# Splitting the first two chunks of the second feed-forward product inside the last group of the first, and loading the next rows one set at a time

## The chip, the cores and the metric

The kernel runs on one core of one Trainium2 chip. The metric is device time in microseconds, the median of three runs. A profile of one further execution was taken with the hardware profiler; its span runs from the first instruction of the program to the last. Engines go by these names: PE or TensorE (matmuls), DVE or VectorE, ACT or ScalarE, POOL or GpSimd, and SP, whose queue issues nearly all DMAs of this kernel.

## What is computed

One layer of a transformer over 2048 latent tokens of width 1024, in 32-bit floats: attention and a gated MLP branch, merged, then a feed-forward sub-layer. The change is in the feed-forward:

```
h2 = modulate(x, norm2_g, sh2, sc2)              # rmsnorm(x, g) * (1 + scale) + shift
x  = x + g2 * (square(relu(h2 @ w_ff1)) @ w_ff2) # w_ff1: 1024 x 4096, w_ff2: 4096 x 1024
```

## The kernel before, in words

**Precision.** Every 32-bit operand `a` of a product is split into a high part in a shorter format (`fp32r`), which ScalarE casts, and the remainder `a - high`, which VectorE subtracts. A product is then three matmuls: high by high, high by low, low by high (`product`, lines 1286 to 1288).

**Seven products instead of eight.** Both feed-forward products work on 2 x 2 blocks of operands and form them from seven block products (Strassen-Winograd); the sums and differences of blocks are made on VectorE. The results accumulate in PSUM banks; some of the seven add on to a bank that another has filled, once that bank was read or rewritten.

**Two blocks.** The 2048 tokens go in two blocks of 1024 (`blk` 0 and 1). For each, `ff1` runs 16 groups (`ff1_group`), each of 7 products of 12 matmuls; the seven combined activations of each group go out to DRAM (`ao_d`, lines 1314 to 1344). During block 0, `w2_late` also forms the seven combinations of the second weights, a slice per group, and stores them (`w2o_d`, `w2_ops`, lines 1259 to 1273); the last group does two slices. Then `ff2` runs 7 x 8 = 56 steps: for each of the seven products, in the order 0, 1, 5, 6, 4, 2, 3, eight chunks `c`, each with four token tiles `t`, 24 matmuls in all.

**A chunk's way.** `ff2_fetch` loads the two operands of a chunk from DRAM (line 1382), 512 KB each, into two buffers of the tag `f4`. `ff2_split` casts each into a further `f4` buffer (ScalarE, line 1391) and subtracts in place (VectorE, line 1392). A chunk thus takes four buffers once split; there are 12 (`"f4": 12`). The weights of a first group use the same tag. Before the loop of `ff2`, chunk 0 is split and chunks 1 and 2 are being loaded; step `n` begins by splitting chunk `n + 1`, then issues the load of chunk `n + 3`, then multiplies chunk `n`.

**After the eighth chunk of a product** (`c == NCH - 1`), `take` evicts each token tile's sum: product 0, 5 and 6 are copied out by ScalarE; product 1 is multiplied by the gate on VectorE (`leave`), after which ScalarE writes product 0's sum back into the bank (line 1437); products 4 and 2 are added to a running sum on VectorE and multiplied by the gate; product 3 is multiplied. Products 0, 1, 5, 6 and 3 share one set of four banks, 4 and 2 the other. `leave` puts the remaining work on the output rows (adding the residual, loaded at line 1413, and the store at line 1426) on a list `late`, from which the next steps take two entries each.

**The side work.** While block 0 is in `ff2`, `h_ops(1, ...)` prepares the first products' operands for block 1: it loads rows of `x` in four sets of four DMAs (`h_fetch`, line 1063, tag `f8`), scales them on VectorE by the inverse root mean square (`h_rstd`, `h_scaled`, line 1070), transposes them on TensorE (`h_turn`, line 184) and makes the seven combinations. It is a generator that advances once at the end of each step. 

**What sets the order.** A planner of the framework orders each engine's instructions by its own costs. `order` adds links that hold parts of it to the order in which the program writes them: all of `ff2` on every engine (`steady`, and `loads` for SP), single stretches (`pins`), and for each tag the order in which buffers are first written. The groups of `ff1` are left to the planner. Engines work through their queues in order, so an instruction that waits holds all that stands behind it.

Of the kernel before, what the change touches and what calls it, by code (L numbers as in the profile page):

```python
# [10 lines left out]
F32R = mybir.dt.float32r  # L11
I32 = mybir.dt.int32
AF = mybir.ActivationFunctionType
ALU = mybir.AluOpType
# [6 lines left out]
KC = D // P  # L21
# [8 lines left out]
TB = 512  # L30
# [16 lines left out]
def f32(ap):  # L47
    return ap.bitcast(F32)
# [20 lines left out]
class Kern:  # L69
# [1012 lines left out]
    def h_ops(self, blk, ops):  # L1082
        nc = self.nc
        add, sub = ALU.add, ALU.subtract
        at = self.here()
        rb = self.h_rstd(blk)
        self.pins.append(range(at, self.here()))
        x = [self.h_fetch(blk, kk) for kk in range(2)]
        yield
        for kk in range(KC // 2):  # L1090
            self.h_scaled(x[kk], rb)
            yield
            raw = {}
            for j in range(2):
                for i in range(2):
                    raw[i, j] = self.h_turn(x[kk], kk, i, j)
                if j and kk + 2 < KC // 2:
                    x.append(self.h_fetch(blk, kk + 2))
                yield
            tt = nc.vector.tensor_tensor  # L1100
            r00, r01, r10, r11 = (raw[i, j] for i in range(2) for j in range(2))
            s1 = self.sb("f2", [TB])
            ops[0][kk] = self.halves(kk, 0, r00)
            tt(out=s1, in0=r10, in1=r11, op=add)
            tt(out=r10, in0=r00, in1=r10, op=sub)
            tt(out=r00, in0=s1, in1=r00, op=sub)
            ops[5][kk] = self.halves(kk, 5, r00)
            yield
            ops[1][kk] = self.halves(kk, 1, r01)
            tt(out=r00, in0=r01, in1=r00, op=sub)  # L1110
            ops[6][kk] = self.halves(kk, 6, r10)
            yield
            ops[4][kk] = self.halves(kk, 4, s1)
            ops[3][kk] = self.halves(kk, 3, r11)
            ops[2][kk] = self.halves(kk, 2, r00)
            yield
# [230 lines left out]
    def ff1(self, blk, h, extra):  # L1347
        w = {0: {}}
        first = self.w1_ops(0, w[0])
        rest = iter(()) if blk else self.h_rest()  # L1350
        if blk == 0:
            for it in (first, rest, rest, first):
                next(it)
        else:
            for _ in first:
                pass
        for g in range(NG):
            nxt = iter(())
            if g + 1 < NG:
                w[g + 1] = {}  # L1360
                nxt = self.w1_ops(g + 1, w[g + 1])
            else:
                raw = self.ff2_fetch(blk, 0, 0)
                self.ready = [self.ff2_split(raw)]
                self.raws = [self.ff2_fetch(blk, 0, 1)]
            more = extra(g)
            for n, _ in enumerate(self.ff1_group(blk, g, w.pop(g), h)):
                next(rest, None)
                if n == 3:
                    next(first, None)  # L1370
                next(nxt, None)
                next(more, None)
            for _ in nxt:
                pass
            for _ in more:
                pass

    def ff2_fetch(self, blk, p, c):
        out = []
        for src in (self.ao_d[blk][p][c], self.wo_d[p][c]):  # L1380
            l = self.sb("f4", [2, TB], F32R)
            self.nc.sync.dma_start(f32(l), src.rearrange("s p c -> p s c"))
            out.append(l)
        return out

    def ff2_split(self, raw):
        nc = self.nc
        out = []
        for l in raw:
            h = self.sb("f4", [2, TB], F32R)  # L1390
            nc.scalar.copy(h, f32(l))  # L1391
            nc.vector.tensor_tensor(out=l, in0=f32(l), in1=f32(h), op=ALU.subtract)  # L1392
            out.append((h, l))
        return out

    def ff2(self, blk, side):
        nc = self.nc
        add, mult = ALU.add, ALU.mult
        begin = self.here()
        ready = self.ready  # L1400
        raws = self.raws + [self.ff2_fetch(blk, 0, 2)]
        late = []

        def tt(out, in0, in1, op):
            nc.vector.tensor_tensor(out=out, in0=in0, in1=in1, op=op)

        goes = {1: (0, 0), 4: (1, 1), 2: (0, 1), 3: (1, 0)}
        u2, u3, xs = ([None] * TT for _ in range(3))

        def residual(p, t):  # L1410
            i, j = goes[p]
            xs[t] = self.sb("f2", [TB])
            nc.sync.dma_start(
                xs[t], self.x1_d[2 * blk + i][t * P : (t + 1) * P, j * TB : (j + 1) * TB]
            )

        def leave(p, t, src):
            i, j = goes[p]
            row = (2 * blk + i) * TB + t * P
            cs = slice(j * TB, (j + 1) * TB)  # L1420
            c, x = self.sb("f2", [TB]), xs[t]
            tt(c, src, self.g2b[:, cs], mult)

            def rest():
                tt(c, c, x, add)
                nc.sync.dma_start(self.out[0, row : row + P, cs], c)

            late.append(rest)

        def take(p, t):  # L1430
            ps = banks[p][t]
            if p == 0:
                u2[t] = self.sb("f2", [TB])
                nc.scalar.copy(u2[t], ps)
            elif p == 1:
                leave(p, t, ps)
                nc.scalar.copy(ps, u2[t])
            elif p in (5, 6):
                u = u2 if p == 5 else u3
                u[t] = self.sb("f2", [TB])  # L1440
                nc.scalar.copy(u[t], ps)
            elif p in (4, 2):
                u = u3[t] if p == 4 else u2[t]
                tt(u, u, ps, add)
                leave(p, t, u)
            else:
                leave(p, t, ps)

        order = (0, 1, 5, 6, 4, 2, 3)
        steps = [(p, c) for p in order for c in range(NCH)]  # L1450
        banks = {}
        for n, (p, c) in enumerate(steps):
            if raws:
                ready.append(self.ff2_split(raws.pop(0)))
            if n + 3 < len(steps):
                raws.append(self.ff2_fetch(blk, *steps[n + 3]))
            (ah, al), (wh, wl) = ready.pop(0)
            fresh = p in (0, 4)
            if c == 0 and fresh:
                new = [self.bank([TB]) for _ in range(TT)]  # L1460
                for other in (0, 1, 5, 6, 3) if p == 0 else (4, 2):
                    banks[other] = new
            if c >= NCH - TT and p in goes:
                residual(p, c - (NCH - TT))
            for t in range(TT):
                if late and t % 2 == 0 and c < NCH - 1:
                    late.pop(0)()
                tok = slice(t * P, (t + 1) * P)
                a = [(ah[:, s, tok], al[:, s, tok]) for s in range(2)]
                b = [(wh[:, s], wl[:, s]) for s in range(2)]  # L1470
                self.product(banks[p][t], a, b, fresh and c == 0)
                if c == NCH - 1:
                    take(p, t)
            next(side, None)
        for f in late:
            f()
        for _ in side:
            pass
        self.loads.append(range(begin, self.here()))
        self.steady.append(range(begin, self.here()))  # L1480
# [336 lines left out]
```

## Time and profile before

| what | value |
|---|---|
| median of three runs | 3013.18 us (3012.45 to 3016.2) |
| the profiled execution | 3012.34 us, of which the span is 3010.6 us |
| granted TensorE clock, mean | 0.999 |
| TensorE busy (matmuls) | 2971.5 us, 99% of the span |
| VectorE busy | 2024.5 us, 67% |
| ScalarE busy | 1353.1 us, 45% |
| DMA | 485.53 MB, 161 GB/s over the span |
| last group of first products, block 0 | 2050.47 to 2070.04 us |
| second products, block 0 and block 1 | from 2070.04 and from 2697.96 us |

Times in the profile are microseconds from the start of the span. A row of a timeline shows start, duration, engine (with q: its instruction queue), line, operation and tiles (written <- read, buffer numbers left out); in square brackets stands how long the engine was idle before and what ended the wait. A matmul is shown with a modelled end: each takes 0.39 us in the records though they start every 0.23 us.

### The profile page before, as it was taken

To read this page: it belongs to the slowest core of one execution; us is meant where nothing else is said; L and a number is where in the kernel's file an instruction comes from. 1 tells how busy PE (TensorE), PEld (TensorE's weight loads), DVE (VectorE), ACT (ScalarE), POOL (GpSimd) and SP (SyncE) were. 2 spreads that over 40 slices of the span, in tenths; PEclk is the share of its full clock that TensorE was granted. 3 is DMA by queue.
4 is the path that set the end of the run, shared out by engine and by line. 5 is a ranking of instruction groups with operands and counts; after the bars stand their busy time and mean duration, and the time that the engine had idled before them with its cause. 6 is when DMAs were issued, how large, how long until landed. Compare 5 with 4: busy or idle time off the path is not lost.

```text
span 3010.6 us, 39824 instructions
## 1 busy us (share of the span) xinstructions
PE 2971.5 (99%) x14973; PEld 2300.4 (76%) x14973; DVE 2024.5 (67%) x2989; ACT 1353.1 (45%) x2041; POOL 564.9 (19%) x420
## 2 busy tenths in 40 slices
PE   7999999999999999999999999999999999999999
PEld 5888888887655656556888878887788888888887
DVE  5848566585777788886655688776755766654455
ACT  4444435342655555554322355443543344444442
POOL 0000000000888899980000000000000000000000
PEclk9999999999999999999999999999999999999999
DMA  7474646643100000003755549888766544446665
GB/s 239 124 219 118 225 137 198 180 138 98 36 15 12 15 19 22 29 26 131 234 174 179 173 151 328 310 305 312 243 203 226 183 154 154 154 148 219 209 218 195
DMA packets 329123, 485.53 MB, mean 161 GB/s; under 512 B 28825, under 2 KB 161217, under 8 KB 328930
## 3 DMA queue, kind: packets, MB, share of 16 engines
q1 hardware_dynamic: 325090, 478.40, 48.1%
q10 hardware_dynamic: 3840, 4.59, 0.4%
q8 instruction: 117, 1.92, 0.3%
q14 instruction: 76, 0.62, 0.1%
HBM read 348.56 MB, written 134.35 MB: 160 GB/s over the span
## 4 chain that ended last, share of the span: by engine, by line
PE 95%; DVE 2%; DMA 2%; ACT 1%; issue 1%; SPq 0%; DVEq 0%; ACTq 0%
PE b L1287 13%; PE b L1288 13%; PE b L1286 13%; PE b L178 11%; PE b L180 11%; PE b L179 11%; PE b L1689 9%; PE b L1709 8%; PE b L1645 2%; PE b L184 2%; DMA w<-in_w_mod 1%; PE b L1751 0%; PE b L288 0%; DMA f<-x_d 0%; DVE ts L1656 0%
## 5 line engine op out<-in xcount | busy, mean ns | idle before, releaser
L1392 DVE TENSOR_TENSOR f<-f,f 128x1024 fp32r<-128x1024 f32 x224 | 264.5, 1221 | 252.7 <-ACT f L1391 252.4
L1656 DVE TENSOR_REDUCE ts<-b 128x1 f32<-128x512 f32 x512 | 311.6, 682 | 105.6 <-PE b L1645 105.5
L1287 PE MATMUL b<-f,f 128*128 128x512 f32 x896 | 350.6, 391 | 5.5 <-DVE f L1392 5.3
L1391 ACT CAST f<-f 128x1024 fp32r<-128x1024 f32 x224 | 224.8, 1052 | 287.3 <-PE b L1287 274.8
L1286 PE MATMUL b<-f,f 128*128 128x512 f32 x896 | 350.2, 391 | 1.3 <-ACT f L1391 1.3
L1288 PE MATMUL b<-f,f 128*128 128x512 f32 x896 | 349.4, 390 | 0.0
L1689 PE MATMUL b<-t,t 64*128 64x512 f32 x2304 | 330.7, 400 | 0.0
L1689 PEld LDWEIGHTS b<-t,t 64*128 64x128 f32 x2304 | 226.1, 184 | 69.2 <-issue 26.1
L1732 POOL TENSOR_TENSOR ac<-ac,p 128x512 f32<-128x512 f32 x204 | 269.0, 1353 | 43.4 <-ACT p L1699 43.4
L1732 POOL TENSOR_TENSOR ac<-ac,t 128x512 f32<-128x512 f32 x146 | 233.2, 1627 | 0.0
L1699 ACT ACTIVATE p<-b 128x512 f32<-128x512 f32 x384 | 206.8, 599 | 48.2 <-PE b L1689 41.4
L1287 PE MATMUL b<-hl,f 128*128 128x512 f32 x576 | 224.4, 390 | 1.8 <-DVE hl L1049 1.8
L1288 PE MATMUL b<-hl,f 128*128 128x512 f32 x576 | 224.1, 389 | 0.0
L1286 PE MATMUL b<-hl,f 128*128 128x512 f32 x576 | 224.1, 389 | 0.0
L150 DVE TENSOR_TENSOR w<-w,w 128x1024 fp32r<-128x1024 f32 x120 | 146.7, 1223 | 113.5 <-ACT w L146 85.7
L178 PE MATMUL b<-t,w 128*128 128x512 f32 x512 | 203.2, 397 | 0.4 <-DVE ts L1651 0.3
L1287 PEld LDWEIGHTS b<-f,f 128*128 128x128 f32 x896 | 168.5, 188 | 44.1 <-DVE f L1392 9.5
L180 PE MATMUL b<-t,w 128*128 128x512 f32 x512 | 199.7, 390 | 0.0
L179 PE MATMUL b<-t,w 128*128 128x512 f32 x512 | 199.5, 390 | 0.0
L1286 PEld LDWEIGHTS b<-f,f 128*128 128x128 f32 x896 | 168.6, 188 | 37.3 <-ACT f L1391 2.4
L1288 PEld LDWEIGHTS b<-f,f 128*128 128x128 f32 x896 | 168.6, 188 | 34.7
L146 ACT CAST w<-w 128x1024 fp32r<-128x1024 f32 x120 | 125.9, 1049 | 146.5 <-DMA w<-in_w_in 116.8
(234 smaller groups left out, 6013.3 us busy)
## 6 DMA issues: line engine op xcount, KB each, us to landing
w<-in_w_in SPq DMA_DIRECT2D x120, 512.0 KB
ao_d<-f SPq DMA_DIRECT2D x224, 256.0 KB
f<-ao_d SPq DMA_DIRECT2D x112, 512.0 KB
f<-w2o_d SPq DMA_DIRECT2D x112, 512.0 KB
f<-in_w_ff SPq DMA_DIRECT2D x48, 1024.0 KB
w2o_d<-f SPq DMA_DIRECT2D x112, 256.0 KB
md<-in_w_mod SPq DMA_DIRECT2D x32, 512.0 KB
f<-x_d SPq DMA_DIRECT2D x64, 256.0 KB
```

Of the source, the lines that this page charges most:

```text
L178: mm(ps, sh, mh, start=start, stop=False, skip_group_check=skip)
L179: mm(ps, sh, ml, start=False, stop=False, skip_group_check=skip)
L180: mm(ps, sl, mh, start=False, stop=stop, skip_group_check=skip)
L1286: mm(ps, wh, hh, start=start and k == 0, stop=False, skip_group_check=True)
L1287: mm(ps, wh, hl, start=False, stop=False, skip_group_check=True)
L1288: mm(ps, wl, hh, start=False, stop=k == len(w) - 1, skip_group_check=True)
L1391: nc.scalar.copy(h, f32(l))
L1392: nc.vector.tensor_tensor(out=l, in0=f32(l), in1=f32(h), op=ALU.subtract)
L1656: nc.vector.tensor_reduce(out=self.mx[:, t, h, c : c + 1], in_=ps[h], axis=AX.X, op=ALU.max)
L1689: self.nc.tensor.matmul(ps[h], keys[h], q[rows[h]], start=n == 0, stop=n == len(steps) - 1, skip_group_check=True,)
L1709: nc.tensor.matmul(self.o[h * HD : (h + 1) * HD, :], k.V[c][:, i, self.kv * HD : (self.kv + 1) * HD], pt[h], start=j == 0, stop=j == NKT - 1,)
L1732: nc.gpsimd.tensor_tensor(out=self.acc[e][:, h], in0=old[:, h], in1=pt[h], op=ALU.add)
```

## The change

Three things are changed, with no change in what is computed.

- In the last group of `ff1` the planner no longer orders the instructions of TensorE, VectorE and ScalarE: the whole group joins `steady`. Inside it a new generator, `ff2_first`, loads the second products' chunks 0 and 1 after the group's first product and splits one operand of them (`ff2_half`: a cast and a subtraction) after each of the next four. `ff2` so begins with two chunks ready and none loaded; its loop, which splits one chunk and loads one per step, is as before, and so is the number of buffers.
- `h_ops` loads one set of rows at a time: the first when it starts, each further one after the scaling of the set before it. Before, two sets were loaded at the start and each further one two ahead. The inverse root mean square of block 1 is computed in group 2 of block 0's first products, not at the start of `h_ops`.
- In `ff2` the side work does not advance at the end of a step in which output rows are still on the list `late`.

```diff
@@ def h_ops(self, blk, ops)
-        at = self.here()
-        rb = self.h_rstd(blk)
-        self.pins.append(range(at, self.here()))
-        x = [self.h_fetch(blk, kk) for kk in range(2)]
+        rb = self.rb1
+        x = [self.h_fetch(blk, 0)]
         yield
         for kk in range(KC // 2):
             self.h_scaled(x[kk], rb)
+            if kk + 1 < KC // 2:
+                x.append(self.h_fetch(blk, kk + 1))
             yield
             raw = {}
             for j in range(2):
                 for i in range(2):
                     raw[i, j] = self.h_turn(x[kk], kk, i, j)
-                if j and kk + 2 < KC // 2:
-                    x.append(self.h_fetch(blk, kk + 2))
                 yield
@@ def ff1(self, blk, h, extra)
         for g in range(NG):
-            nxt = iter(())
+            begin = self.here()
             if g + 1 < NG:
                 w[g + 1] = {}
                 nxt = self.w1_ops(g + 1, w[g + 1])
             else:
-                raw = self.ff2_fetch(blk, 0, 0)
-                self.ready = [self.ff2_split(raw)]
-                self.raws = [self.ff2_fetch(blk, 0, 1)]
+                nxt = self.ff2_first(blk)
+            if g == 2 and blk == 0:
+                self.rb1 = self.h_rstd(1)
...
             for _ in more:
                 pass
+        self.steady.append(range(begin, self.here()))
+
+    def ff2_first(self, blk):
+        self.ready, self.raws = [], []
+        raws = [self.ff2_fetch(blk, 0, c) for c in range(2)]
+        for raw in raws:
+            got = []
+            for l in raw:
+                yield
+                got.append(self.ff2_half(l))
+            self.ready.append(got)
+
+    def ff2_half(self, l):
+        h = self.sb("f4", [2, TB], F32R)
+        self.nc.scalar.copy(h, f32(l))
+        self.nc.vector.tensor_tensor(out=l, in0=f32(l), in1=f32(h), op=ALU.subtract)
+        return h, l
@@ def ff2_split(self, raw)
-        nc = self.nc
-        out = []
-        for l in raw:
-            h = self.sb("f4", [2, TB], F32R)
-            nc.scalar.copy(h, f32(l))
-            nc.vector.tensor_tensor(out=l, in0=f32(l), in1=f32(h), op=ALU.subtract)
-            out.append((h, l))
-        return out
+        return [self.ff2_half(l) for l in raw]
@@ def ff2(self, blk, side)
-            next(side, None)
+            if not late:
+                next(side, None)
```

## The prediction

> **What bounds the kernel now.** I read the page, then what TensorE waited for, then, around those waits, the timelines of the four queues.
>
> ```profile
> span 3010.6 us, 39824 instructions
> PE 2971.5 (99%) x14973; PEld 2300.4 (76%) x14973; DVE 2024.5 (67%) x2989; ACT 1353.1 (45%) x2041; POOL 564.9 (19%) x420
> ```
>
> TensorE is the bound, so only two things count: waits of TensorE that vanish, and waits that are new. In the part that the change touches (two blocks, each 16 groups of first products and 56 steps of second products) its timeline shows these waits:
>
> ```profile
> 2076.06 0.50 PE L1286 MATMUL b<-f,f 128*128 128x512 f32 x1 [0.42 <-ACT f L1391]
> 2078.38 0.50 PE L1287 MATMUL b<-f,f 128*128 128x512 f32 x1 [1.81 <-DVE f L1392]
> 2084.86 0.50 PE L1287 MATMUL b<-f,f 128*128 128x512 f32 x1 [0.70 <-DVE f L1392]
> 2091.13 1.09 PE L184 MATMUL b<-ident,f 128*128 128x128 f32 x8 [0.75 <-DVE f L1070]
> 2093.40 0.50 PE L1287 MATMUL b<-f,f 128*128 128x512 f32 x1 [0.94 <-DVE f L1392]
> 2181.43 0.50 PE L1286 MATMUL b<-f,f 128*128 128x512 f32 x1 [0.88 <-ACT f L1391]
> 2182.88 0.50 PE L1287 MATMUL b<-f,f 128*128 128x512 f32 x1 [0.95 <-DVE f L1392]
> 2704.83 0.50 PE L1287 MATMUL b<-f,f 128*128 128x512 f32 x1 [0.94 <-DVE f L1392]
> ```
>
> The bracket is idle time after a modelled end; as these ends overlap, each wait costs some 0.2 us more. Block 0's entry into the second products loses 4.6 + 5 x 0.2 = 5.6 us, the place at 2181 1.8 + 0.4 = 2.2, block 1's entry 1.1. After the second of them the clock was halved for one stretch:
>
> ```profile
> 2180.20:2183.60 3.40, 1.57 (x6) 0.82 (x5) 3.15 (x5) 3.40 (x6) 0.00 (x0) 1.00 0.45 172
> 2183.60:2187.00 3.40, 3.40 (x10) 2.63 (x9) 3.40 (x6) 2.29 (x4) 0.00 (x0) 0.50 0.79 240
> 2074.40:2077.80 3.40, 1.74 (x7) 0.89 (x5) 3.40 (x5) 1.61 (x2) 0.00 (x0) 1.00 0.97 369
> 1802.80:1821.90 19.10, 19.10 (x86) 15.80 (x85) 15.24 (x22) 11.02 (x17) 0.00 (x0) 1.00 0.85 296
> ```
>
> Columns: stretch, length, busy TensorE, weight loads, VectorE, ScalarE, GpSimd, granted clock. A stretch with TensorE busy 1.57 of 3.40 us was followed by 3.4 us at 0.50; one with 1.74 was not. Half of 3.4 us is 1.7; the halved stretch runs 10 matmuls instead of the next one's 16, 6 x 0.23 = 1.4: some 1.6 us lost. So at most 5.6 + 2.2 + 1.6 + 1.1 = 10.5 us can be won.
>
> **The steady step.** A step is 24 matmuls; from 2742.81 to 2786.33, the starts of steps 8 and 16 of block 1, is 8 steps, 5.44 us each.
>
> ```profile
> 2050.47 0.39 PE L1286 MATMUL b<-he,f 128*128 128x512 f32 x1
> 2678.92 0.39 PE L1286 MATMUL b<-he,f 128*128 128x512 f32 x1
> 2710.40 0.39 PE L1287 MATMUL b<-f,f 128*128 128x512 f32 x1
> 2742.81 0.39 PE L1286 MATMUL b<-f,f 128*128 128x512 f32 x1
> 2786.33 0.39 PE L1286 MATMUL b<-f,f 128*128 128x512 f32 x1
> ```
>
> ```profile
> 2075.48 1.02 SPq L1273 DMA_DIRECT2D w2o_d<-f  x2
> 2076.59 0.41 SPq L1382 DMA_DIRECT2D f<-ao_d  x1
> 2078.64 9.15 SPq L1063 DMA_DIRECT2D f<-x_d  x8
> 2702.61 0.41 SPq L1382 DMA_DIRECT2D f<-ao_d  x1
> 2715.80 0.36 SPq L1382 DMA_DIRECT2D f<-ao_d  x1
> ```
>
> ```profile
> 2082.49 1.06 ACT L1391 CAST f<-f 128x1024 fp32r<-128x1024 f32 x1 [0.18 <-DMA f<-w2o_d]
> 2694.11 0.63 ACT L1300 ACTIVATE f<-f 128x512 f32<-128x512 f32 x1
> 2707.73 1.05 ACT L1391 CAST f<-f 128x1024 fp32r<-128x1024 f32 x1 [0.20 <-DMA f<-w2o_d]
> 2715.58 2.01 ACT L1391 CAST f<-f 128x1024 fp32r<-128x1024 f32 x2 [3.43 <-PE b L1287]
> 2737.34 2.01 ACT L1391 CAST f<-f 128x1024 fp32r<-128x1024 f32 x2 [3.43 <-PE b L1287]
> 2739.25 0.58 ACT L1434 COPY f<-b 128x512 f32<-128x512 f32 x1
> 2784.95 1.79 ACT L1437 COPY b<-f 128x512 f32<-128x512 f32 x3 [2.08 <-DVE f L1405]
> ```
>
> ```profile
> 2075.37 0.68 DVE L1270 TENSOR_TENSOR f<-f,f 128x512 f32<-128x512 f32 x1
> 2078.24 0.16 DVE L156 TENSOR_SCALAR fs<-ss 128x8 f32<-128x8 f32 x1
> 2081.09 0.17 DVE L173 TENSOR_TENSOR fs<-fs,fs 128x8 f32<-128x8 f32 x1
> 2695.44 0.69 DVE L1296 TENSOR_TENSOR f<-f,b 128x512 f32<-128x512 f32 x1 [2.03 <-PE b L1288]
> 2707.57 2.47 DVE L1392 TENSOR_TENSOR f<-f,f 128x1024 fp32r<-128x1024 f32 x2 [2.80 <-ACT f L1391]
> 2781.95 2.36 DVE L1392 TENSOR_TENSOR f<-f,f 128x1024 fp32r<-128x1024 f32 x2 [3.08 <-ACT f L1391]
> 2912.51 2.36 DVE L1392 TENSOR_TENSOR f<-f,f 128x1024 fp32r<-128x1024 f32 x2 [3.07 <-ACT f L1391]
> 2914.78 0.68 DVE L1405 TENSOR_TENSOR f<-f,b 128x512 f32<-128x512 f32 x1
> ```
>
> All four queues follow the written order here. At the head of step n, ScalarE and VectorE split a chunk; further down the same queues stand the evictions that step n's own sums need. The split starts the moment TensorE releases a chunk (2715.58, ended by PE): its data has long landed, and only its buffers were missing. The load goes out 0.2 us into the step (2715.80). All 12 buffers `f4` are in use.
>
> **Part 1: both chunks split early.** The loop is unchanged, but it now starts with two chunks ready and one load out, so at step n it splits chunk n+2 (before n+1) and loads n+3. Wanted at once: chunks n, n+1, n+2 split (4 buffers each) and load n+3 (2), which is 14; there are 12. The split comes first in the order of buffers, so load n+3 has to wait for chunk n: it goes out at the end of step n, one step later than before. And the split at the head of step n is of a chunk whose load went out 0.2 us after that step began. ScalarE and VectorE therefore wait in every step for a load in flight, and the evictions stand behind.
>
> How late: block 1's first split on fresh data gives it. Load issued 2702.61, second cast 2707.73 to 2708.78 (6.17 us later), subtractions done 2707.57 + 2.47 = 2710.04 (7.43). With the 0.2, ScalarE is done 6.4 us into a step, VectorE 7.6. Before: casts 2737.34 + 2.01 in a step begun at 2742.81 - 5.44 = 2737.37, done at 2.0; subtractions 2784.31 in the one begun at 2780.89, done at 3.4. So the evictions come 4.4 us later on ScalarE, 4.2 on VectorE. Chunks themselves stay in time (7.6 against two steps, 10.9). On SP the waiting load holds the residual rows' loads and the output writes behind it up to a step; both are wanted a step later at the earliest, so 0. Block 0's turning of the next rows stands behind the split too, with more than a step to spare.
>
> That hits TensorE at the four passages per block where the next product accumulates on a bank just evicted; the other two go to banks long free. Margins before:
> - 0 to 1: copy done 2739.83, next step 2742.81, margin 3.0; new wait 4.4 - 3.0 = 1.4.
> - 1 to 5: VectorE, then the copy back, the first of three done 2784.95 + 0.6 = 2785.55; next step 2786.33, margin 0.8; new wait 4.2 - 0.8 = 3.4.
> - 5 to 6: as 0 to 1, 1.4; in block 0 eight transposes stand before it (0.8) and leave 0.6.
> - 4 to 2: the addition done 2915.46, next step 2786.33 + 24 x 5.44 = 2916.89, margin 1.4; new wait 2.8.
> Together 9.0 in block 1, 8.2 in block 0: **+17.2**. Bounds: with the load of block 0's entry (2076.59 to 2082.49, 5.9 instead of 5.1) 0.8 more at eight passages, 23.6; had the second load landed 0.2 sooner, its cast would have followed the first at once, 8 x 0.2 less, 15.6.
>
> **Part 2: the entries.** The waits at 2076 to 2078 and at 2704 go, since chunk 1 is ready. But chunk 2 is next, and its load stands on SP behind the last writes of the first products, hence behind VectorE. In the written order four casts and subtractions stand between the sums. Block 1: the fourth cast follows an activation done at 2694.74; 1.05 + 1.22 later is 2697.0, and only then comes the sum that ran at 2695.44: 1.5 later, and all behind it, the load too (2704.1). Chunk 2 is split at 2710.04 + 1.5 = 2711.5; it was used at 2710.40. **+1.2**: the wait moves one step on and grows. Block 0 has the additions for the second weights besides (lines 1266 to 1270, two sets of four, 0.7 each), written between the sums. The load waits for the last (2075.37 on, then 2075.48 on SP). Its delay lies between 1.5 and 1.5 + 4 x 0.7 = 4.3, and I take 2.8, as half of these stand ahead in any order. Against it the wait at 2093.40 (1.2) goes: chunk 3's split now precedes the scaling of the next rows. **+1.6**, between 0 and 3.
>
> **Part 3: next rows a set at a time.** Four loads instead of eight at 2078.64 (some 4.6 us of SP fewer ahead of the next chunk's load), and each later set goes out six steps ahead of its use: hidden, 0; if not hidden, one wait like the 0.75 at 2091.13, which I leave in. The rsqrt chain (2078.24 to 2081.26, 3.0 us of VectorE) moves to group 2 of block 0; there VectorE was busy 15.2 of 19.1 us, so 3.9 us cover it: 0, at worst 3.
>
> **Part 4: no side work while output rows are pending.** At 2181 side work delayed the output rows, their writes held SP, and a chunk's load came late; without it this goes: **-2.2 and -1.6** for its clock.
>
> **Part 5: the clock.** By the two stretches above, a wait that leaves TensorE under about half busy in such a stretch is followed by 1.6 us lost. Waits of 3.4 do that wherever they fall (2), those of 2.8 mostly (1.5 of 2), block 0's entry (over 5 together) once: 4.5 x 1.6 = **+7.2**, between 0 and 8 x 1.6 = 12.8.
>
> Sum: 17.2 + 1.2 + 1.6 - 3.8 + 7.2 = 23.4 on the profiled execution's 3012.34 us (0.8 below the median shown): **3036**.
>
> **Rivals.**
> [...]
> - Not slower: the load's buffers are free a step sooner than I count, so the data is there at the step's head. It decides where subtractions end by 3.4 + 0.8 = 4.2 us into a step: no passage waits and no clock falls. Left are 1.2 + 1.6 - 3.8 = -1.0: 3011. For it: SP and ScalarE do overlap with TensorE everywhere before; against it: the split before waits for exactly these buffers (2715.58).
> - Everything intended happens, chunk 2 in time too, so that all 10.5 go: 3002. That needs the load at 2702.61 at least 1.3 us sooner, though it stands behind later writes.
> - Loads come slower still, or other evictions cross a step: 3050.
>
> **How the numbers follow.** Forecast 0.57, clock stays 0.23, not slower 0.10, all won 0.07, worse 0.03. The likeliest's own range is 3025 (15.6 + 1.2 + 0 - 3.8, no clock term) to 3046 (between 3044, with 23.6 + 1.2 + 3 - 3.8 + 7.2, and 3049, with 12.8 for the clock); to leave out no more than 2 in 10 I go down to 3012, into the third case. Under 0.2% (6 us) cannot be told from no change; faster 0.07, same 0.11, slower 0.82.
>
> **What would show it.** Right: loads at line 1382's successor issued at the end of each step; casts ended by a DMA and not by PE in steady steps; waits of TensorE on ScalarE or VectorE after steps 7, 15, 23 and 39 of each block; granted clock 0.50 behind them; nothing at 2181. Wrong: casts still ended by PE in steady steps, or TensorE without waits at these passages.

## Result and profile after

The changed kernel takes 3033.04 us, median of 4 runs (3032.24 to 3034.86), against 3012.89 us for the kernel before, also of 4 runs. The ratio is 1.0066, with a 95% interval of 1.0054 to 1.0079: slower by 20 us, where 23 were forecast. The profiled execution took 3032.24 us, of which the span is 3030.5, 19.9 more than before. The mean granted clock fell from 0.999 to 0.996.

In the changed kernel the matmuls of a product stand in lines 1284 to 1286, the cast and the subtraction of a split in 1389 and 1390, the load of a chunk in 1397; the evictions are 1442 (product 0), 1445 (the copy back after product 1), 1449 (products 5 and 6) and 1413 (all of VectorE's work on the second products' sums: the multiplication by the gate, and the additions of products 4 and 2).

From the page of the profile after: the span, the busy time, and the engines' shares of the chain of work that ended last.

```profile
span 3030.5 us, 39816 instructions
PE 2976.8 (98%) x14973; PEld 2305.0 (76%) x14973; DVE 2030.3 (67%) x2989; ACT 1363.4 (45%) x2041; POOL 564.7 (19%) x420
PE 90%; DMA 4%; DVE 2%; ACT 2%; issue 1%; SPq 0%; DVEq 0%; ACTq 0%
```

TensorE has as many matmuls as before; the time is waiting and a lower clock. Where it lies is seen by cutting both spans into stages: first products and second products of block 0, then of block 1. Each row gives the stretch, its length and the busy time of TensorE, weight loads, VectorE and ScalarE (with counts), GpSimd, the granted clock, the share of DMA and GB/s. Before:

```profile
1758.83:2070.04 311.21, 307.68 (x1346) 251.23 (x1344) 246.43 (x333) 153.47 (x227) 0.00 (x0) 1.00 0.84 295
2070.04:2393.32 323.28, 316.68 (x1409) 259.23 (x1408) 201.16 (x224) 148.69 (x176) 0.00 (x0) 0.99 0.67 229
...
2697.96:3004.22 306.26, 305.31 (x1345) 251.83 (x1343) 154.40 (x150) 120.16 (x128) 0.00 (x0) 1.00 0.63 214
```

After:

```profile
1759.54:2072.28 312.74, 308.06 (x1345) 251.19 (x1344) 249.92 (x349) 153.97 (x227) 0.00 (x0) 1.00 0.83 293
2072.28:2399.73 327.45, 314.78 (x1410) 259.59 (x1409) 200.84 (x208) 153.69 (x176) 0.00 (x0) 0.99 0.66 226
...
2704.37:3024.13 319.76, 311.28 (x1345) 255.11 (x1343) 155.83 (x148) 123.78 (x128) 0.00 (x0) 0.98 0.59 205
```

The first products of block 0 lose 1.5 us, the second products of block 0 4.2 and those of block 1 13.5; the first products of block 1, left out here, take 304.64 us in both. The first row also shows 16 more instructions on VectorE (349 for 333), the next one 16 fewer.

TensorE's waits at the entries and behind them, after (start, duration, engine, line, operation; in brackets the idle time and what ended it). Each entry has a second wait, for a subtraction, of 0.47 and 0.76 us, not shown here:

```profile
2089.11 0.79 PE L1284 MATMUL b<-f,f 128*128 128x512 f32 x1 [5.79 <-ACT f L1389]
2127.14 0.50 PE L1284 MATMUL b<-f,f 128*128 128x512 f32 x1 [1.05 <-ACT f L1442]
2176.80 0.50 PE L1284 MATMUL b<-f,f 128*128 128x512 f32 x1 [3.14 <-ACT b L1445]
2312.56 0.47 PE L1284 MATMUL b<-f,f 128*128 128x512 f32 x1 [2.22 <-DVE f L1413]
2716.59 0.50 PE L1284 MATMUL b<-f,f 128*128 128x512 f32 x1 [1.18 <-ACT f L1389]
2752.63 0.50 PE L1284 MATMUL b<-f,f 128*128 128x512 f32 x1 [0.59 <-ACT f L1442]
2799.21 0.50 PE L1284 MATMUL b<-f,f 128*128 128x512 f32 x1 [2.77 <-ACT b L1445]
2845.54 0.50 PE L1284 MATMUL b<-f,f 128*128 128x512 f32 x1 [0.89 <-ACT f L1449]
2935.19 0.47 PE L1284 MATMUL b<-f,f 128*128 128x512 f32 x1 [2.28 <-DVE f L1413]
```

Two entries (2089 and 2716) and seven passages, the passages each at the first matmul of a product and ended by the eviction that the forecast named. Nothing is left at 2181. As modelled ends overlap, start to start a wait is 0.16 to 0.17 us more than its bracket: the seven passages cost 12.9 + 7 x 0.16 = 14.1 us.

How the step changed is seen on ScalarE's waits in block 1's second products. The columns are the waiting line, what it waited for, us in total, how often, the longest. Before, from 2715 to 2995:

```profile
ACT f L1391 <- PE b L1287: 157.9, 47, 3.5
```

After, from 2720 to 3000, and the two queues in the last step of product 0 (it began at 2752.63 - 0.76 - 5.44 = 2746.43):

```profile
ACT f L1389 <- DMA f<-ao_d: 155.9, 48, 7.8
...
2746.40 0.36 SPq L1397 DMA_DIRECT2D f<-ao_d  x1
2749.85 2.24 ACT L1389 CAST f<-f 128x1024 fp32r<-128x1024 f32 x2 [2.93 <-DMA f<-ao_d]
2752.00 2.04 ACT L1442 COPY f<-b 128x512 f32<-128x512 f32 x4
```

The split waits as often and as long in all as before (47 times 3.4 us, 48 times 3.2), but for another thing: once for TensorE to let a chunk's buffers go, now for a load in flight. And it waits at another place. The casts that were done 2.0 us into a step end at 2752.09, 5.7 us into it; the copy of product 0 behind them starts at 2752.00 and not at 2739.25 - 2737.37 = 1.9 us into its step. The load goes out at 2746.40, when the step before has ended.

The granted clock (rows of stretches, columns as above):

```profile
2082.80:2086.20 3.40, 0.52 (x3) 0.10 (x1) 0.00 (x0) 0.00 (x0) 0.00 (x0) 1.00 0.91 277
2086.20:2093.00 6.80, 3.42 (x7) 2.43 (x8) 4.88 (x4) 4.18 (x4) 0.00 (x0) 0.50 1.09 380
2174.90:2178.30 3.40, 1.50 (x7) 1.24 (x8) 3.02 (x5) 2.12 (x4) 0.00 (x0) 1.00 1.07 404
2714.20:2717.60 3.40, 1.71 (x7) 0.85 (x5) 2.26 (x2) 2.61 (x3) 0.00 (x0) 1.00 1.04 387
2796.20:2799.60 3.40, 0.63 (x4) 0.34 (x3) 3.40 (x5) 1.50 (x3) 0.00 (x0) 1.00 0.54 191
2799.60:2803.00 3.40, 3.40 (x10) 2.63 (x9) 1.77 (x3) 3.26 (x5) 0.00 (x0) 0.50 0.50 195
2932.70:2936.10 3.40, 1.12 (x5) 0.81 (x5) 3.37 (x5) 0.49 (x1) 0.00 (x0) 1.00 0.61 208
```

Four times in this part the clock is halved, to 0.50, from 2086.2, 2717.7, 2799.6 and 2936.1 us on: behind both entries, and in block 1 behind the passages 1 to 5 and 4 to 2. The halved stretch behind 2086.2 lasts 6.8 us, the others 3.4. The longest passage of all, 3.14 us at 2176.80, was not followed by it.

### The profile page after: what moved, and what is told of

It reads as the page before. It is cut to its first block, busy times and chain, and to the rows that moved or that the text cites. A ratio compares the mean times of both kernels' runs of the same rounds, so it can differ in the third digit from the quotient of the medians.

```text
span 3030.5 us, 39816 instructions
## 1 busy us (share of the span) xinstructions
PE 2976.8 (98%) x14973; PEld 2305.0 (76%) x14973; DVE 2030.3 (67%) x2989; ACT 1363.4 (45%) x2041; POOL 564.7 (19%) x420
## 4 chain that ended last, share of the span: by engine, by line
PE 90%; DMA 4%; DVE 2%; ACT 2%; issue 1%; SPq 0%; DVEq 0%; ACTq 0%
PE b L1284 11%; PE b L1285 11%; PE b L178 11%; PE b L1286 11%; PE b L180 11%; PE b L179 11%; PE b L1698 9%; PE b L1718 8%; DMA f<-w2o_d 3%; PE b L1654 2%; PE b L184 2%; ACT f L1389 1%; DMA w<-in_w_mod 1%; DVE f L1294 1%; PE b L1760 0%
## 5 line engine op out<-in xcount | busy, mean ns | idle before, releaser
L1390 DVE TENSOR_TENSOR f<-f,f 128x1024 fp32r<-128x1024 f32 x224 | 271.3, 1225 | 281.8 <-ACT f L1389 280.7
L1389 ACT CAST f<-f 128x1024 fp32r<-128x1024 f32 x224 | 235.1, 1052 | 322.9 <-DMA f<-ao_d 302.1
L1284 PE MATMUL b<-f,f 128*128 128x512 f32 x896 | 352.6, 393 | 19.9 <-ACT f L1389 7.0
```

The lines of the kernel that those rows point to most:

```text
L1284: mm(ps, wh, hh, start=start and k == 0, stop=False, skip_group_check=True)
L1389: self.nc.scalar.copy(h, f32(l))
L1390: self.nc.vector.tensor_tensor(out=l, in0=f32(l), in1=f32(h), op=ALU.subtract)
```

## Experiments

The theory: the loss comes from the place of the split in the queues. It stands ahead of the evictions and waits for a load that goes out a step late, because two chunks split ahead need 14 buffers and there are 12. The main rivals: the late data itself is the loss, or the split inside the last group, or the clock alone. Experiments 1 to 4 had 27 runs of the kernel before beside them (median 3012.99 us), 5 to 7 had 23 (3013.33), 8 had 10 (3012.68).

### 1. Evictions ahead of the split

On the changed kernel, in the last step of each product the split and the next load are written behind the evictions; loads stay as late as they are.

```
+            def ahead():
+                if raws:
+                    ready.append(self.ff2_split(raws.pop(0)))
+                if n + 3 < len(steps):
+                    raws.append(self.ff2_fetch(blk, *steps[n + 3]))
+
+            if c < NCH - 1:
+                ahead()
...
+            if c == NCH - 1:
+                ahead()
             if not late:
                 next(side, None)
```

> The changed kernel, but in the last step of each product (steps 7, 15, 23 and so on) the split and the next load stand behind the step's evictions in the queues, not ahead of them; nothing else differs, so the loads still go out at the end of a step. Theory A (evictions queue behind a split that waits for a load in flight): the waits of TensorE at the passages go, 14.3 us of new waits plus some 3.2 us of halved clock behind them, so 3033 - 17.5 = about 3015.5 us; the entries stay. Rival B (the loads, one step later, starve TensorE itself or the queue SP is the cause): the passages keep waiting, 3033.

Measured: 3018.96 us (3015.47 to 3022.32, 10 runs), ratio 1.0021 (1.0012 to 1.003). The waits of ScalarE from 2725 to 3000, of TensorE from 2120 to the end of block 1, and the stage of block 1's second products:

```profile
ACT f L1389 <- DMA f<-ao_d: 140.4, 46, 5.6
...
PE b L1285 <- DVE f L1390: 2.8, 4, 0.9
PE b L1284 <- ACT f L1389: 1.4, 1, 1.4
PE b L184 <- issue: 0.8, 1, 0.8
...
2703.41:3012.51 309.10, 306.97 (x1345) 253.12 (x1343) 156.19 (x148) 124.40 (x128) 0.00 (x0) 0.99 0.61 212
```

The split still waits for loads in flight, 46 times, yet no line of an eviction is left among what TensorE waits for, and block 1 is at 309.10 instead of 319.76 us. So data that comes a step late costs little by itself; it costs through the evictions queued behind it. What is left over the kernel before is the entry of block 1 with its clock (2.8 us), and in block 0 2.0 us in the first products and 2.7 in the second (325.99 us), with an entry wait of 6.3 us and three short waits for a subtraction. The time is 3.5 us above the 3015.5 expected: in the profiled execution the granted clock is 0.99 in the first products of block 0 (1.00 in the changed kernel) and 0.98 in the second (0.99), where behind the entry's wait the matmuls from 2092.02 to 2094.58 start every 0.43 us and not every 0.23.

### 2. Split one chunk ahead, as before

```
-            if raws:
+            if raws and len(ready) < 2:
                 ready.append(self.ff2_split(raws.pop(0)))
```

In step 0 nothing is split; from then on a chunk is split one step ahead, and two split chunks (8 buffers), one that is loaded (2) and a load under way (2) fit into 12. The split inside the last group stays.

> The changed kernel with one condition added: step n splits a further chunk only when fewer than two are ready. So step 0 splits nothing and from step 1 on the loop is that of the kernel before: loads three steps ahead, 12 buffers suffice. Theory A: no wait at the passages, casts in steady steps ended by TensorE again; the entries stay as in the changed kernel (chunk 2 late in both blocks), the wait at 2181 stays away: about 3014.5. Rival B' (what costs is the last group's written order or the rows loaded a set at a time, not the split two ahead): near 3033.

Measured: 3016.56 us (3011.93 to 3020.42, 10 runs), ratio 1.0011 (1.0002 to 1.0021). Its profiled execution is the lowest of the ten. ScalarE's main wait from 2715 to 2995, the copy back at the passage 1 to 5 of block 1, and both stages of second products:

```profile
ACT f L1389 <- PE b L1285: 158.5, 47, 4.0
...
2784.53 1.79 ACT L1445 COPY b<-f 128x512 f32<-128x512 f32 x3 [2.08 <-DVE f L1413]
...
2070.05:2391.71 321.66, 315.95 (x1410) 259.61 (x1409) 197.36 (x208) 148.27 (x176) 0.00 (x0) 0.99 0.66 230
2696.34:3003.80 307.46, 305.51 (x1345) 251.83 (x1343) 152.60 (x148) 119.21 (x128) 0.00 (x0) 1.00 0.62 213
```

One condition gives the steady step back: casts are released by TensorE again, the copy back has the same idle time ahead of it as in the kernel before (2.08 us, ended by VectorE), and of the passages only 1 to 5 of block 0 still waits, 0.21 us. Against the changed kernel the two stages win 5.8 and 12.3 us. Block 1's stage still stands 1.2 us over that of before: its entry, the forecast's +1.2, now alone. That the median lies 4.6 us above this profiled execution, more than in other kernels, is not explained by the trace; it stays open.

### 3. No side work while rows are pending, alone

On the kernel before, only `if not late:` ahead of `next(side, None)`.

> The kernel before with the third part alone: no side work in steps with output rows pending. If the wait at 2181 and its halved clock come from the side work ahead of the output rows, both go: 3012.9 - 4.6 = 3008.3. If the wait had another cause (the transposes, the load of the next rows): no change, 3012.9.

Measured: 3009.89 us (3008.44 to 3011.17, 11 runs), ratio 0.9989 (0.998 to 0.9998). The stretch where the wait at 2181 stood, and block 0's second products:

```profile
2180.40:2183.80 3.40, 3.40 (x20) 2.91 (x20) 0.06 (x1) 2.48 (x4) 0.00 (x0) 1.00 0.91 296
2071.38:2390.79 319.41, 314.73 (x1410) 258.10 (x1409) 201.16 (x224) 149.13 (x176) 0.00 (x0) 1.00 0.67 231
```

TensorE is busy throughout, and the stage wins 323.28 - 319.41 = 3.9 us; 3.8 was forecast for this part. The median is 1.6 us above the 3008.3 expected: the place at 2181 with its clock is gone, some 4.5 us, but a wait at the passage 1 to 5 of block 0 is new and takes some 0.5 back, and the first products of block 0 take 311.73 us, 0.5 more than before.

### 4. Room for two chunks split ahead

On the changed kernel, two buffers more of `f4`, paid with one of `f8`.

```
-    "early": {"f8": 3, "f2": 16, "he": 20, "fs": 5},
-    "late": {"hl": 36, "f4": 12},
+    "early": {"f8": 2, "f2": 16, "he": 20, "fs": 5},
+    "late": {"hl": 36, "f4": 14},
```

> The changed kernel with 14 buffers for chunks in place of 12; to make room, the tag of the rows and of the raw weights has 2 buffers in place of 3. Theory A: 14 is what the split two ahead wants, so loads go out at the head of a step three ahead again and the passages' waits (14.3 us and 3.2 of clock) go: about 3015.5 plus whatever the lost buffer costs in the first products, which is read from that stretch alone (0 to 10). Rival B'' (the split two ahead costs by its place in the queues, whatever the buffers): passages wait as in the changed kernel, 3033 or more.

Measured: 3028.28 us (3026.49 to 3031.75, 4 runs), ratio 1.0053 (1.0039 to 1.0067). The stages of first and second products of block 0, second products of block 1, and ScalarE's main wait from 2730 to 3010:

```profile
1759.38:2084.81 325.43, 312.81 (x1346) 252.91 (x1344) 248.70 (x351) 153.55 (x227) 0.00 (x0) 0.98 0.79 281
2084.81:2405.97 321.16, 314.10 (x1409) 259.68 (x1408) 201.11 (x212) 149.85 (x177) 0.00 (x0) 0.99 0.66 228
2711.59:3019.02 307.43, 305.36 (x1345) 251.99 (x1343) 153.26 (x148) 120.04 (x128) 0.00 (x0) 1.00 0.61 213
...
ACT f L1389 <- PE b L1285: 138.3, 43, 3.4
```

The second products, still splitting two chunks ahead, take what they take in experiment 2 (321.16 and 307.43 us against 321.66 and 307.46): with 14 buffers the split waits for TensorE again and the passages cost next to nothing (0.2 us at one of them). So the price is the missing two buffers, as counted. The time as a whole says little on that, since the smaller `f8` loses 14.2 us in the first products of block 0 against the kernel before, most of it at their start, where TensorE waits 4.3 and 5.2 us and the clock is at 0.50 for 13.6 us (1768.00 to 1781.60).

### 5. Chunks 2 and 3 loaded inside the last group

On experiment 2, both loads are written at the end of `ff2_first`, step 0 loads nothing, and the next rows' first set is scaled two steps later.

```
+        self.raws = [self.ff2_fetch(blk, 0, c) for c in (2, 3)]
...
-        raws = self.raws + [self.ff2_fetch(blk, 0, 2)]
+        raws = self.raws
...
-            if n + 3 < len(steps):
+            if n and n + 3 < len(steps):
```

> The kernel of the held split (no split in step 0), with the loads of chunks 2 and 3 also issued inside the last group of the first products, ahead of its last writes on SP, and the side work begun with its first load in step 0 but its scaling two steps later (step 3). If the waits left at the entries come from chunk 2's load standing behind the last writes, and in block 0 from the first rows behind that load, both entries are free: block 0's second products lose 6.6 us of waits and some 1.2 of halved clock, block 1's 2.4, so 3016.6 - 10 = about 3006.5. Rival: the entries wait for the splits' own place in the written order (VectorE's backlog at the end of the group), and the waits stay whatever the loads do: 3016.

Measured: 3005.53 us (3001.98 to 3006.47, 8 runs), ratio 0.9972 (0.9961 to 0.9982). The stages of second products:

```profile
2070.87:2384.63 313.76, 313.59 (x1409) 258.28 (x1408) 197.18 (x208) 147.83 (x176) 0.00 (x0) 1.00 0.68 234
2689.27:2994.20 304.93, 304.93 (x1345) 251.92 (x1343) 152.42 (x148) 119.05 (x128) 0.00 (x0) 1.00 0.61 211
```

TensorE is busy throughout. The 9.5 and 1.3 us that the kernel before lost at its entries and at 2181 are thus won, once nothing waits for what comes after the split. They aren't the split's alone: of the 9.5, experiment 3 by itself wins 3.9 and experiment 7 1.9, and the later scaling of the next rows was not tried by itself.

### 6. The inverse root mean square back in its place

On experiment 5, computed and pinned at the start of `h_ops` again.

> The same with the inverse root mean square of block 1 back where the kernel before had it, at the start of the side work in step 0, in place of the first products. If its chain of 15 small VectorE operations costs the wait at 1764 (1.97 in place of 0.70 us), 1.3 us less than the run with the loads in the group, about 3005; and in step 0 it costs nothing, as chunk 1 is ready by then. Rival: the wait at 1764 has another cause, or the chain costs as much in step 0: no difference.

Measured: 3005.88 us (3004.73 to 3010.19, 10 runs), ratio 0.9975 (0.9966 to 0.9984). The second products of block 0, and TensorE's wait in them with VectorE's work ahead of it (here the subtraction is line 1393 and the matmul 1289):

```profile
2069.95:2387.96 318.01, 315.01 (x1409) 259.52 (x1408) 199.51 (x223) 147.71 (x176) 0.00 (x0) 0.99 0.67 230
2081.81 4.63 DVE L1393 TENSOR_TENSOR f<-f,f 128x1024 fp32r<-128x1024 f32 x4
2084.22 0.50 PE L1289 MATMUL b<-f,f 128*128 128x512 f32 x1 [3.00 <-DVE f L1393]
```

A miss: the chain was expected to cost nothing in step 0. The first products win 1.2 us (310.77), but the chain occupies VectorE from 2078.88 to 2081.81, the subtractions of chunks 2 and 3 stand behind it, and TensorE waits 3.2 us: it is busy 1.38 of 3.40 us from 2082.20 on, and the clock of the next 3.40 us is 0.50. The second products lose 4.2 us.

### 7. Next rows a set at a time, alone

On the kernel before, only the change in `h_ops` and the inverse root mean square of block 1 in group 2.

> The kernel before with the second part alone: rows loaded a set at a time, the inverse root mean square computed among the first products. I expect +1.3 us in the first products of block 0 (the wait at 1764 grows) and up to 1 us less at the entry of block 0 (four row loads fewer ahead of chunk 4's load, the chain of small operations out of the way), the wait at 2181 as before: 3013 to 3014. Rival: this part carries a gain or loss of several us by itself: under 3010 or over 3017.

Measured: 3014.76 us (3011.92 to 3016.86, 11 runs), ratio 1.0004 (0.9995 to 1.0012): no difference that can be told. The first products of block 0, and VectorE and TensorE at their start:

```profile
1759.01:2071.52 312.51, 308.75 (x1346) 252.62 (x1344) 249.11 (x348) 153.70 (x227) 0.00 (x0) 0.99 0.83 294
1761.84 0.17 DVE L156 TENSOR_SCALAR fs<-ss 128x8 f32<-128x8 f32 x1 [1.22 <-ACT jk L1038]
1766.05 0.80 PE L1286 MATMUL b<-he,f 128*128 128x512 f32 x1 [1.81 <-DVE f L1242]
```

Two effects cancel. The chain is written in group 2, but the planner, which orders that group, puts it at 1761.84, ahead of the first one. The chain ends at 1764.86, the subtraction that the first group waits for (line 1242) starts only then, and the wait of 0.53 us that TensorE had there before is 1.81: the stage loses 1.3 us. In the second products (321.38 us) VectorE no longer has the chain, the waits of 0.70 and 0.75 us at 2084.86 and 2091.13 are gone, and 1.9 us are won; the halved clock is still there, but behind the entry (0.50 from 2080.0 on) and not behind the wait at 2181.

### 8. The inverse root mean square held in group 8

On experiment 5, the chain is written behind the fourth product of group 8 of block 0 (`n == 3`), and pinned behind that product's evictions, so that the planner can't put it ahead of them.

```
+            at = self.here()
             for n, _ in enumerate(self.ff1_group(blk, g, w.pop(g), h)):
+                if g == 8 and n == 3 and blk == 0:
+                    self.rb1 = self.h_rstd(1)
+                    self.pins.append(range(at, self.here()))
...
+                at = self.here()
```

> Chunks 2 and 3 loaded inside the last group, split one step ahead, and the inverse root mean square held inside group 8 of block 0's first products, behind that group's third product, where VectorE has idle time. Theory (the 1.3 us lost at 1764 come from the planner, which hoisted the chain ahead of the first group): the wait at 1764 falls back from 1.97 to 0.70 us, group 8 shows no wait, and the step 0 to 1 of the second products keeps none: 1.3 us less than with the chain ahead of the first group, 3004.2 against 3005.5, and block 0's first products 310.7 instead of 312.0 us. Rival (the forecast's worst for this part: the chain isn't covered wherever it stands): up to 3 us of waiting in group 8, block 0's first products 312 to 314 us.

Measured: 3002.79 us (3001.09 to 3003.82, 6 runs), ratio 0.9967 (0.9955 to 0.9979), the lowest of all kernels here. The same stages of block 0, and the chain's first instruction:

```profile
1759.32:2069.92 310.60, 307.29 (x1345) 251.38 (x1344) 247.59 (x349) 154.26 (x227) 0.00 (x0) 1.00 0.84 297
2069.92:2383.36 313.44, 313.38 (x1409) 258.34 (x1408) 197.10 (x208) 147.86 (x176) 0.00 (x0) 1.00 0.67 234
1931.14 0.16 DVE L156 TENSOR_SCALAR fs<-ss 128x8 f32<-128x8 f32 x1
```

The chain runs from there to 1942.96, its operations between those of the other work, and TensorE waits nowhere in that time: the first products take 310.60 us against 311.98 in experiment 5. The two kernels' intervals overlap, so that this 1.4 us rests on the traces and not on the times.

## Why the prediction was right, and where its sizes were off

The forecast of 3036 us stands against 3033; direction, mechanism and places are those of the likeliest case. Term by term, on the profiled executions (the clock's cost is what remains of each step's delay after its waits: step 16 of block 1 takes from 2799.21 to 2806.41, 7.2 us instead of 5.44):

| term | forecast, us | measured, us |
|---|---|---|
| seven or eight passages | +17.2 | +14.1 |
| entry of block 0 | +1.6 | +1.3 |
| entry of block 1 | +1.2 | +1.2 |
| next rows' sets and inverse root mean square | 0 | +1.5 |
| place at 2181, with its clock | -3.8 | -4.5 |
| clock | +7.2 | +6.0 |
| short waits elsewhere in the second products | none | -0.4 |
| ahead of the first products | none | +0.7 |
| sum | +23.4 | +19.9 |

The short waits: three for a subtraction in block 0, 0.27 us each, are gone, and against them stands some 0.1 us behind each passage.

That the sum came this near is in part luck: the passages, the clock and the place at 2181 came out 5.0 us under the forecast together, and the chain and what lies ahead of the first products, forecast at nothing, 2.2 over it.

**Part 1** holds. The count of 14 buffers against 12 is borne out by experiment 4, the place in the queue by experiment 1, and the cure of both by experiment 2. Its size was off by 3.1. I took 6.17 us from a load's issue to its second cast from block 1's first split on fresh data, where the second load landed after a gap; in the steady step the casts run in one go and end at 2749.85 + 2.24 = 2752.09, 5.7 us after the issue at 2746.40. That is the forecast's lower bound of 15.6 and a little less. The one passage missing, 5 to 6 in block 0, was put at 0.6; the eight transposes ahead of it covered all of it.

**Part 2** holds. In block 0 the chunk's load went out at 2081.94, 9.7 us into the second products instead of 6.6 (2076.59): 3.1 later, 2.8 forecast. Its waits add to 5.79 + 0.16 and some 1.0 for the subtraction behind, 7.0 where before stood 5.6. The wait of 0.9 on the transposes at 2091.13, which I had left in, went too. In block 1 they are 2.4 instead of 1.2.

```profile
2081.94 0.41 SPq L1397 DMA_DIRECT2D f<-ao_d  x1
```

This row of the changed kernel is the end of the chain of the forecast: the last addition for the second weights is done at 2081.30, their writes are issued from 2080.96 on, and the load stands behind them.

**Part 3** failed in one step: "moves to group 2 of block 0; there VectorE was busy 15.2 of 19.1 us, so 3.9 us cover it". The first half is what the program writes, not what the planner did; it ran the chain of 15 operations at 1762 (in experiment 7 from 1761.84 on, in the changed kernel from 1762.37 on). There it cost 1.3 of the 1.5 us, inside the bound of 3. Experiment 8 shows that idle time does cover the chain where it is held in place.

**Part 4** holds, in the changed kernel and alone (experiment 3).

**Part 5** holds in that the clock was halved behind stretches in which TensorE was partly busy, and its count is near by luck: 4.5 halvings were forecast, there were 4, but not where they were put. "Waits of 3.4 do that wherever they fall" failed: of these two, put down as sure, one did not come (3.3 us at 2176.80). Of the two passages 4 to 2 one had it, and the entry of block 1, for which the forecast counted none, had it too. "Clock stays", given 0.23, did not come: the four halvings follow stretches in which TensorE was busy 0.52, 1.71, 0.63 and 1.12 us of 3.40.

Of the other rivals, "all won" is worth a word: its 3002 us were not had by this change, but they were there. Experiment 8, at 3002.79, comes to this time with what the change lacked: no split further ahead than the buffers allow, and chunk 2's load ahead of the last writes; it also scales the next rows two steps later and holds the chain in group 8.

## What to carry to other kernels

Before something is prepared one step earlier in a loop, count the buffers that the deeper state holds at its widest point; if they are too few, the next load moves a step back, and here the queues passed its delay on to what is written behind its first use, above all to the work that frees the accumulators (the copy of product 0 started 5.6 us into its step instead of 1.9). A prologue that fills the pipeline deeper than the loop can hold should be followed by a step that takes nothing in (one condition won back 16.5 us of the median here, and 18 us in the second products of the profiled executions). And code moved into a stretch that a planner orders goes where the planner puts it: read its place in the trace, or pin it behind something that can't move.

## What the hardware showed

For how a partly idle TensorE and a halved clock go together, the forecast had two stretches of the kernel before. The traces show more of them, and the busy time alone does not part them. Stretches of 3.40 us with TensorE busy 0.52, 0.63, 1.12 and 1.71 us (changed kernel, from 2082.80, 2796.20, 2932.70 and 2714.20 on), 1.38 us (experiment 6, from 2082.20 on) and 1.57 us (before, from 2180.20 on) were followed by a clock of 0.50. Stretches with 1.00 and 1.50 us (changed kernel, from 2174.40 and 2174.90 on, at the passage at 2176.80) and with 1.74 us (before, from 2074.40 on) were not. The entry of block 0 shows it best: before, its waits of 0.42 and 1.81 us left TensorE busy 1.16 us from 2075.12 to 2078.52, and the next 3.40 us stood at 1.00, while in experiment 7 the same two waits left the same 1.16 us and the clock was halved:

```profile
2076.60:2080.00 3.40, 1.16 (x5) 0.43 (x4) 3.20 (x4) 0.89 (x1) 0.00 (x0) 1.00 0.96 341
2080.00:2083.40 3.40, 3.40 (x9) 2.66 (x10) 0.31 (x1) 1.14 (x2) 0.00 (x0) 0.50 0.97 354
```

The length of a wait does not part them either: the passage at 2176.80, 3.3 us long, kept its clock, and the one at 2799.21, 2.9 us long, lost it. What parts them was not shown, so that a count of halvings taken ahead from the waits is an estimate. The four of the changed kernel cost 1.5 to 1.75 us in each of the three in block 1, and some 1.1 in the 6.8 us of block 0's entry, which were mostly waiting anyway.
